# mLSTM gate arithmetic placed in the projection stage instead of attention, with eager evacuations, five raw buffers and shifted attention splits

## The chip, the cores and the metric

The kernel runs on 1 core of a Trainium2 chip. The metric is the device time of one execution in microseconds (us). Engines are named as in the profile: PE is the matmul engine (PEld its weight load), DVE the vector engine, ACT the scalar engine with its function tables, POOL the general engine, SP the engine whose queue issues nearly all DMAs here. PSUM is the memory that PE writes its products to.

## What is computed

One encoder layer on x of 2048 tokens by 1024 features, all in float32:

```python
h = rms_norm(x);  z = h @ W_in      # columns: mLSTM q|k|v|out-gate|16 gates, MLA latents, rotary key
qk  = silu(conv5(z_q|z_k))          # centred convolution over 5 tokens
y_a = sigmoid(o) * rms_norm(mlstm_fwd(q,k,v,i,f) + mlstm_bwd(...))   # 4 heads, chunks of 128 tokens
y_b = attention(4 heads, per-head RMSNorm on q and k, rotary part of 64)
x = x + concat(y_a, y_b) @ W_out
x = x + relu(rms_norm(x) @ W1)**2 @ W2
# mLSTM, per head and direction, before any product with q, k, v:
b = cumsum_in_chunk(log_sigmoid(f));  u = i - b;  cu = cummax(u)
m = running state over the 16 chunks (max/add);  M = max(cu, m)
w = exp(u - M_last);  it = exp(m - M);  gd = exp(-(b + M));  dec = exp(m - M_last)
```

The last three lines are the gate arithmetic, which this change moves. Its whole input is the 16 gate columns for 2048 tokens (c.G, 128 partitions); everything is 128 x 128 or smaller.

## The kernel before

Every float32 product is made of three PE matmuls of high and low parts (lines 68 to 70, `mm3`), so each operand is split: ACT casts the high part (L53), DVE or POOL subtracts the low part (L54). For the weights of the first stage, which also take a gain, L56 is ACT's cast and L57 DVE's low part.

Stages, in order of time:

- **Projection** (`phase_a`, 0 to 466 us). Two halves of 1024 tokens. A half begins with the 464 columns of gates and latents (`rest`: gate evacuation into c.G, L284 `zr`), and then come three blocks of eight products each: blk 0 is `z_v` (mLSTM values), blk 1 `z_qk` (transposed q and k, then the convolution), blk 2 `z_o` (output gate). Each product is 24 matmuls of 512 columns into one of two banks (`pz`, pool psZ), evacuated into `vo` or `zc`. Weights come as `raw` tiles (pool `a_raw`, 3 buffers), 8 to a block. Between them run the MLA steps (`tick`: latent norms, `cTh` splits, the k, v, q products into `pm`, transpositions of `kn`, `qn`, `qr`, `kr` into `pt`, stores of kT, qT, rT). `prep` transposes x into hh and hl. The order of instructions in this stage is not the order of the code: a tile scheduler sets it by priorities (code order, unless a block is marked with a priority offset), against its own model of the engines.
- **Attention** (`attention`, 467 to 1165 us). The order is written by hand: step g of 256, eight (s = 0 to 7) to each block of 256 queries, emits score, softmax, transposition and value products, and calls `next(work)` once on the mLSTM generator, which therefore fills the steps one yield at a time. That generator begins with `mlstm_prelude` (24 yields, the gate arithmetic), then `mlstm_steps`. The prelude's small matmuls and transpositions on PE go through `pm` banks, its arithmetic through DVE and ACT. `split_q` and `split_k` (ACT cast, POOL or DVE low parts) prepare the next queries and the next head.
- **Output projection and feed-forward** (from about 1160 us to the end): a hand-written order, where `weights()` splits W_out during attention's last steps, and `load_y(s)`, `load_x(s)` bring tile s of y and x into a ring of tiles.

All SP DMAs stand in one queue: a DMA that waits for its tile holds all behind it.

Of the kernel before, what the change touches and what calls it, by code (L numbers as in the profile page):

```python
# [8 lines left out]
F32 = mybir.dt.float32  # L9
# [57 lines left out]
def mm3(nc, out, ah, al, bh, bl, first, last):  # L67
    nc.tensor.matmul(out, ah, bh, start=first, stop=False)  # L68
    nc.tensor.matmul(out, ah, bl, start=False, stop=False)  # L69
    nc.tensor.matmul(out, al, bh, start=False, stop=last)  # L70
# [17 lines left out]
def scratch(c, ctx):  # L88
# [15 lines left out]
    c.d_dec = dr.tile([P, 1], F32, name="d_dec")  # L104
# [13 lines left out]
def phase_a(c):  # L118
    nc, tc = c.nc, c.tc
    with ExitStack() as st:  # L120
# [6 lines left out]
        rp = pool("a_raw", 3)  # L127
# [10 lines left out]

        def load_x(t):
            xt = kp.tile([P, D], F32, name=("wukh", "wukl")[t - 2]) if t in (2, 3) else xp.tile([P, D], F32, name="xt")  # L140
            for q, cs in ((nc.sync, slice(0, 512)), (nc.scalar, slice(512, D))) if t == 0 else ((nc.sync, slice(0, D)),):
                q.dma_start(xt[:, cs], c.x[t * P:(t + 1) * P, cs])
            return xt

        def prep(t, xt, hh, hl):

            if t >= NL:
                junk = ep.tile([P, D], BF16, name="xjunk", bufs=1)
# [6 lines left out]
            for g in range(2):  # L155
                pt = psT.tile([P, 4, P], F32, name="pt")
                for k in range(4):
                    nc.tensor.transpose(pt[:, k, :], xt[:, (4 * g + k) * P:(4 * g + k + 1) * P], c.ident)
                split(nc, hh[:, 4 * g:4 * g + 4, tt * P:(tt + 1) * P],
                      hl[:, 4 * g:4 * g + 4, tt * P:(tt + 1) * P], pt)  # L160
# [104 lines left out]
        def z_nat(hts, tl, w, n):  # L265
# [3 lines left out]
            for k in range(KD):  # L269
                mm3(nc, pz[:, :n], hh[:, k, ts], hl[:, k, ts], w[k][0][:, :n], w[k][1][:, :n],  # L270
                    k == 0, k == KD - 1)
            return pz

        def rest(t, hts, w):
            pz = z_nat(hts, t % 8, w, NR)
            for half, ci in ((0, t), (2, NT - 1 - t)):
                dst, zg, b = c.G[:, half:half + 2, :, ci], pz[:, half * 4:half * 4 + 8].rearrange(
                    "p (a h) -> p a h", a=2), bg[:, half * 4:half * 4 + 8].rearrange("p (a h) -> p a h", a=2)
                if t < NL:
                    nc.vector.scalar_tensor_tensor(dst, zg, rinv[:, t:t + 1], b, op0=ALU.mult, op1=ALU.add)  # L280
                else:
                    nc.vector.tensor_tensor(dst, zg, b, op=ALU.add)
            zr = zp.tile([P, 448], F32, name="zr")
            nc.scalar.activation(zr, pz[:, 16:NR], AF.Copy, scale=rinv[:, t:t + 1] if t < NL else 1.0)  # L284
# [16 lines left out]
        def mla_a1(t, zr):  # L301
# [17 lines left out]
            split(nc, ch, cl, pt[:, 0:3, :])  # L319
# [93 lines left out]
        def z_qk(j, ch, hts, w):  # L413
# [13 lines left out]
            if j == 0:  # L427
                nc.vector.tensor_tensor(zc[:, 4:516], pz, rbs[0], op=ALU.mult)
            else:
                nc.scalar.copy(zc[:, 4:516], pz)  # L430
# [39 lines left out]
        def z_v(t, hts, w):  # L470
            pz = z_nat(hts, t % 8, w, 512)
            o = ep.tile([P, 512], F32, name="vo")
            if t < NL:
                nc.vector.tensor_scalar(o, pz, rinv[:, t:t + 1], None, op0=ALU.mult)
            else:
                nc.vector.tensor_copy(o, pz)
            nc.sync.dma_start(c.d_v[t * P:(t + 1) * P, :], o)

        def z_o(t, hts, w):
            pz = z_nat(hts, t % 8, w, 512)  # L480
            o = ep.tile([P, 512], F32, name="vo")
            nc.scalar.activation(o, pz, AF.Sigmoid, scale=rinv[:, t:t + 1] if t < NL else 1.0)
# [37 lines left out]
        for half in range(2):  # L520
# [34 lines left out]
            for blk in range(3):  # L555
# [3 lines left out]
                for i in range(8):  # L559
# [35 lines left out]
def mlstm_prelude(c, psM):  # L595


    nc, tc = c.nc, c.tc
    H = P // 2
    with ExitStack() as st:  # L600
        pool = st.enter_context(tc.tile_pool(name="g_sb", bufs=1, reuse_waits="tile"))

        def bank():
            return psM.tile([P, 512], F32, name="pm")

        def sb(name, shape=(P, P)):
            return pool.tile(list(shape), F32, name=name)

        pg = bank()[:, 0:256].rearrange("p (a t) -> p a t", a=2)
        for j in range(2):  # L610
            nc.tensor.matmul(pg[0:H, j, :], c.G[:, j], c.ident, start=True, stop=True)
            nc.tensor.matmul(pg[H:P, j, :], c.G[:, 2 + j], c.rev, start=True, stop=True)
        yield
        f, li, e, w, ln, d = sb("f"), sb("li"), sb("e"), sb("w"), sb("ln"), sb("d")
        nc.vector.tensor_copy(f, pg[:, 1, :])
        nc.vector.tensor_copy(li, pg[:, 0, :])
        yield
        nc.scalar.activation(e, f, AF.Abs)
        nc.scalar.activation(e, e, AF.Exp, scale=-1.0)
        yield  # L620
        nc.vector.tensor_scalar(w, e, 1.0, None, op0=ALU.add)
        yield
        wi = sb("wi")
        nc.scalar.activation(ln, w, AF.Ln)
        nc.vector.tensor_scalar(d, w, 1.0, None, op0=ALU.subtract)
        nc.vector.tensor_tensor(d, e, d, op=ALU.subtract)
        nc.vector.reciprocal(wi, w)
        nc.vector.tensor_tensor(d, d, wi, op=ALU.mult)
        yield
        yield  # L630
        nc.vector.tensor_tensor(ln, ln, d, op=ALU.add)
        nc.vector.scalar_tensor_tensor(f, f, 0.0, ln, op0=ALU.min, op1=ALU.subtract)
        b, u, cu, gs = sb("b"), sb("u"), sb("cu"), sb("gs", (P, 2))
        nc.vector.tensor_tensor_scan(b, f, f, 0.0, op0=ALU.add, op1=ALU.bypass)
        yield
        nc.vector.tensor_tensor(u, li, b, op=ALU.subtract)
        nc.vector.tensor_tensor_scan(cu, u, u, -3.0e38, op0=ALU.max, op1=ALU.bypass)
        nc.vector.tensor_copy(gs[:, 0:1], b[:, P - 1:P])
        nc.vector.tensor_copy(gs[:, 1:2], cu[:, P - 1:P])
        yield  # L640
        yield
        yield
        pr = bank()[0:1, 0:256].rearrange("p (a t) -> p a t", a=2)
        for j in range(2):
            nc.tensor.transpose(pr[:, j, :], gs[:, j:j + 1], c.ident)
        yield
        g1, mr = sb("g1", (1, 2, P)), sb("mr", (1, 8, NT))
        nc.vector.tensor_copy(g1, pr)
        nc.vector.memset(mr, 0.0)
        for r in range(8):  # L650
            s = slice(r * NT, (r + 1) * NT - 1)
            nc.vector.tensor_tensor_scan(mr[:, r, 1:], g1[:, 1, s], g1[:, 0, s], 0.0, op0=ALU.max, op1=ALU.add)
        yield
        yield
        pm = bank()[:, 0:1]
        nc.tensor.transpose(pm, mr.rearrange("p r c -> p (r c)"), c.ident[0:1, 0:1])
        yield
        mp = sb("mp", (P, 1))
        nc.vector.tensor_copy(mp, pm)
        M, it, dec, gd, nl = c.gM, c.git, c.gdec, sb("gd"), sb("nl", (P, 1))  # L660
        nc.vector.tensor_scalar(M, cu, mp, None, op0=ALU.max)
        nc.vector.tensor_scalar(nl, M[:, P - 1:P], -1.0, None, op0=ALU.mult)
        nc.vector.tensor_tensor(gd, b, M, op=ALU.add)
        yield
        nc.scalar.activation(dec, mp, AF.Exp, bias=nl)
        nc.scalar.activation(w, u, AF.Exp, bias=nl)
        nc.scalar.activation(it, M, AF.Exp, scale=-1.0, bias=mp)
        nc.scalar.activation(gd, gd, AF.Exp, scale=-1.0)
        nc.sync.dma_start(c.d_dec, dec)
        yield  # L670
        x1, x2 = sb("x1", (P, 3, P)), sb("x2", (P, 2, P))
        p2 = bank()[:, 0:256].rearrange("p (a t) -> p a t", a=2)
        for j, t in enumerate((M, it)):
            nc.tensor.transpose(p2[:, j, :], t, c.ident)
        yield
        nc.vector.tensor_copy(x2, p2)
        p1 = bank()[:, 0:384].rearrange("p (a t) -> p a t", a=3)
        for j, t in enumerate((u, w, gd)):
            nc.tensor.transpose(p1[:, j, :], t, c.ident)
        yield  # L680
        nc.vector.tensor_copy(x1, p1)
        for par in range(2):
            nc.sync.dma_start(
                c.dec[par * 64:(par + 1) * 64],
                c.d_dec.rearrange("(a p c) o -> p o a c", p=2, c=NT)[par].to_broadcast((64, 4, NT)))
        yield
        p4 = bank()[0:H, 0:256].rearrange("p (a t) -> p a t", a=2)
        for j in range(2):
            nc.tensor.matmul(p4[:, j, :], x2[:, j, H:P], c.rev, start=True, stop=True)
        yield  # L690
        rv = c.grv
        nc.vector.tensor_copy(rv, p4)
        p3 = bank()[:, 0:192].rearrange("p (a t) -> p a t", a=3)
        nc.tensor.matmul(p3, c.rev, x1[:, :, H:P], start=True, stop=True)
        yield
        nc.vector.tensor_copy(c.gn[:, :, 0:H], x1[:, :, 0:H])
        nc.vector.tensor_copy(c.gn[:, :, H:P], p3)
        yield
        for d in range(2):
            for h in range(NH):  # L700
                r = slice(d * H + h * NT, d * H + (h + 1) * NT)
                rr = slice(h * NT, (h + 1) * NT)
# [1284 lines left out]
```

## Time and profile before

| | |
|---|---|
| median of 3 runs | 2597.55 us (2594.62 to 2598.93) |
| profiled execution, own time | 2595.53 us |
| its span | 2593.8 us |
| granted TensorE clock | 1.0 |
| PE busy | 2568.8 us (99%) |
| DVE, ACT, POOL busy | 1674.2, 1213.0, 396.0 us (65, 47, 15%) |

The span covers the first to the last instruction; the own time has 1.7 us more around it. Rows of the profile read: line of the kernel, engine, operation, output<-inputs, count, then busy time and mean ns, and the idle time just before with what ended it. In answers in order of time, a row begins with its start and its length in us. Buffer numbers are left out of names.

### The profile page before, as it was taken

The page shows a single profiled execution, that of the slowest core. Times are in us where ns is not written, and L with a number is a line of the kernel's source. Part 1 is how long each engine was busy: PE and PEld are TensorE (multiplying, and loading weights), DVE is VectorE, ACT ScalarE, POOL GpSimd, SP SyncE. Part 2 cuts the span into 40 slices and gives each one's busy share as a digit, 9 for nine tenths or more (in the row PEclk, how much of TensorE's full clock was granted, in tenths as well). Part 3 has the DMA queues.
Part 4 walks back from the last instruction along what each step waited for, and adds up shares of the span by engine and source line. Part 5 has one row for each costly group of instructions (what it writes and reads, how often), then busy time and mean ns, then how long its engine had stood idle before and what let it go on. Part 6 is the DMA issues. An engine that isn't in the chain of part 4 may idle for free. (4 is left out here: it accounts for less than half of the span.)

```text
span 2593.8 us, 37092 instructions
## 1 busy us (share of the span) xinstructions
PE 2568.8 (99%) x13232; PEld 2168.7 (84%) x13232; DVE 1674.2 (65%) x3206; ACT 1213.0 (47%) x2457; POOL 396.0 (15%) x438
## 2 busy tenths in 40 slices
PE   8999999999999999999999999999999999999999
PEld 7888887788888888898888888888888888888887
DVE  5585467666676667675458777877775477675443
ACT  6454444545656556572135554655554323332332
POOL 1111110123224214111000000000000133222000
PEclk9999999999999999999999999999999999999999
DMA  5334235366446555435674656754446644444542
GB/s 168 126 119 151 94 114 164 68 134 126 104 86 131 92 111 105 86 110 173 211 247 160 198 185 195 253 174 142 161 147 241 247 146 146 146 146 146 211 176 97
DMA packets 297757, 391.57 MB, mean 151 GB/s; under 512 B 32677, under 2 KB 186340, under 8 KB 297572
## 3 DMA queue, kind: packets, MB, share of 16 engines
q1 hardware_dynamic: 295108, 384.74, 50.2%
q10 hardware_dynamic: 2464, 4.46, 0.5%
q8 instruction: 104, 1.70, 0.3%
q14 instruction: 81, 0.66, 0.1%
HBM read 256.94 MB, written 132.17 MB: 150 GB/s over the span
## 5 line engine op out<-in xcount | busy, mean ns | idle before, releaser
L68 PE MATMUL pd<-w2h,uh 128*128 128x512 f32 x896 | 348.7, 389 | 0.1
L69 PE MATMUL pd<-w2l,uh 128*128 128x512 f32 x896 | 348.6, 389 | 0.0
L70 PE MATMUL pd<-w2h,ul 128*128 128x512 f32 x896 | 348.6, 389 | 0.0
L54 DVE TENSOR_TENSOR ul<-ur,uh 128x1024 fp32r<-128x1024 f32 x110 | 147.1, 1337 | 252.5 <-ACT uh L53 252.3
L53 ACT CAST uh<-ur 128x1024 fp32r<-128x1024 f32 x110 | 115.9, 1054 | 395.4 <-PE pd L69 381.3
L54 DVE TENSOR_TENSOR ptl<-ptp,pth 128x512 fp32r<-128x512 f32 x252 | 173.7, 690 | 183.0 <-ACT pth L53 176.1
L53 ACT CAST pth<-ptp 128x512 fp32r<-128x512 f32 x252 | 146.4, 582 | 241.7 <-PE ptp L1106 233.2
L1604 DVE TENSOR_TENSOR e<-pu,e 128x512 f32<-128x512 f32 x224 | 151.5, 689 | 98.3 <-PE pu L70 88.9
L1066 DVE TENSOR_SCALAR_CACHE_REDUCE p<-ps 128x512 f32<-128x512 f32 x256 | 174.9, 684 | 44.0 <-PE ps L1065 39.0
L68 PEld LDWEIGHTS pd<-w2h,uh 128*128 128x128 f32 x896 | 168.2, 188 | 35.5 <-DVE e L1604 0.5
L70 PEld LDWEIGHTS pd<-w2h,ul 128*128 128x128 f32 x896 | 168.2, 188 | 34.9
L69 PEld LDWEIGHTS pd<-w2l,uh 128*128 128x128 f32 x896 | 168.2, 188 | 34.9
L1764 POOL TENSOR_TENSOR r<-wr,r 128x512 f32<-128x512 f32 x48 | 85.8, 1788 | 620.8 <-DMA wr<-in_w 594.7
L1480 ACT CAST r<-w1raw 128x512 fp32r<-128x512 f32 x160 | 98.3, 615 | 121.9 <-PE pu L70 112.3
L68 PE MATMUL pz<-wh,hh 128*128 128x512 f32 (+1 forms) x384 | 150.2, 392 | 5.0 <-ACT hh L53 1.8
L1106 PE MATMUL ptp<-ident,p 128*128 128x128 f32 x1008 | 150.9, 273 | 1.3 <-ACT p L1077 0.9
L69 PE MATMUL pz<-wl,hh 128*128 128x512 f32 (+1 forms) x384 | 149.7, 390 | 1.7 <-DVE wl L57 1.6
L70 PE MATMUL pz<-wh,hl 128*128 128x512 f32 (+1 forms) x384 | 150.6, 392 | 0.0
L69 PE MATMUL pv<-ptl,vh 128*128 128x256 f32 x496 | 140.8, 284 | 2.4 <-DVE ptl L54 2.1
L68 PE MATMUL pv<-pth,vh 128*128 128x256 f32 x496 | 140.7, 284 | 0.0
L1607 ACT ACTIVATE e<-e 128x512 f32<-128x512 f32 x128 | 81.0, 633 | 127.1 <-DVE e L1604 120.6
L70 PE MATMUL pv<-pth,vl 128*128 128x256 f32 x496 | 140.3, 283 | 0.0
(441 smaller groups left out, 6587.0 us busy)
## 6 DMA issues: line engine op xcount, KB each, us to landing
d_u<-e SPq DMA_DIRECT2D x224, 256.0 KB
ur<-d_u SPq DMA_DIRECT2D x110, 512.0 KB
w1raw<-in_w SPq DMA_DIRECT2D x64, 512.0 KB
wr<-in_w SPq DMA_DIRECT2D x96, 256.0 KB
raw<-in_w_in SPq DMA_DIRECT2D x48, 256.0 KB
mb<-d_M SPq DMA_DIRECT2D x32, 256.0 KB
r<-in_x SPq DMA_DIRECT2D x16, 512.0 KB
d_x<-r SPq DMA_DIRECT2D x16, 512.0 KB
```

What stands on the lines that cost most here:

```text
L53: nc.scalar.copy(hi, src)
L54: (eng or nc.vector).tensor_tensor(lo, src, hi.bitcast(F32), op=ALU.subtract)
L68: nc.tensor.matmul(out, ah, bh, start=first, stop=False)
L69: nc.tensor.matmul(out, ah, bl, start=False, stop=False)
L70: nc.tensor.matmul(out, al, bh, start=False, stop=last)
L1066: nc.vector.tensor_scalar(probs[b, a][:, j, :], o, SCALE, None, op0=ALU.mult, op1=ALU.max, accum_out=maxes[b, a][:, j:j + 1])
L1106: nc.tensor.transpose(pt[:, k, :], p[:, j, k * P:(k + 1) * P], c.ident)
L1480: self.c.nc.scalar.copy(wh, src)
L1604: nc.vector.tensor_tensor(out, o, t, op=ALU.add)
L1607: nc.scalar.activation(t, t, AF.Relu)
L1764: nc.gpsimd.tensor_tensor(R, wr, R, op=ALU.subtract)
```

## The change

1. `mlstm_prelude` (24 yields in attention) is gone. `gate_arithmetic` does the same arithmetic in the second half of the projection, one step behind each of the eight value products. Its PE steps are put under `issue_after(c.last.ins)`, c.last being the last matmul of the newest z product, and its DVE and ACT work under a priority raised by 400. Its tiles take the slots of `zc`, `ot`, `acc`, `sg`, `kt` in the pool of the convolution (two buffers of zc and ot, one of the others), its PSUM banks come from psT (`pt`, two banks, shared with the transpositions). One transposition more brings `dec` into a row. Results go to DRAM (`d_gn`, 192 KB; `d_dec`; as before d_M and d_in), and attention starts with `load_gates`: three loads, then 4 yields in place of 24. The mLSTM generator therefore runs 20 steps earlier through all of attention.
2. Evacuations of PSUM in the projection stage are marked `urgent()` (priority raised by 400).
3. `a_raw` has 5 buffers instead of 3.
4. In attention, `split_q` is at s = 3 (5 before), `split_k` of parts 1, 2, 3 at s = 4, 6, 7 (4, 5, 6), and the next head's first value loads at s = 7 (6).
5. `load_y(2)` of the output projection is issued inside `weights()`, ahead of `load_x(0)`; before, after the end of attention.

```diff
@@ phase_a
-        rp = pool("a_raw", 3)
+        rp = pool("a_raw", 5)
+        def urgent():
+            return tc.high_priority(offset=400)
...
-                split(nc, hh[:, 4 * g:4 * g + 4, tt * P:(tt + 1) * P],
-                      hl[:, 4 * g:4 * g + 4, tt * P:(tt + 1) * P], pt)
+                with urgent():
+                    split(nc, hh[:, 4 * g:4 * g + 4, tt * P:(tt + 1) * P],
+                          hl[:, 4 * g:4 * g + 4, tt * P:(tt + 1) * P], pt)
...
-            split(nc, ch, cl, pt[:, 0:3, :])
+            with urgent():
+                split(nc, ch, cl, pt[:, 0:3, :])
...
+            with urgent():
+                if j == 0:
+                    nc.vector.tensor_tensor(zc[:, 4:516], pz, rbs[0], op=ALU.mult)
+                else:
+                    nc.scalar.copy(zc[:, 4:516], pz)
...
                     if blk == 0:
                         z_v(t0 + i, hts, w)
+                        if half == 1:
+                            if i == 0:
+                                gates = gate_arithmetic(c, ep, psT)
+                            next(gates, None)
@@ gate_arithmetic (new; the arithmetic as in mlstm_prelude)
+    (f, li, e, w), tf = four("zc")
+    (ln, d, wi, b), _ = four("zc")
+    (u, cu, M, it), _ = four("ot")
+    (gd, _, _, sm), tg = four("ot")
...
+    gn = tf[:, 0:3 * P].rearrange("p (a t) -> p a t", a=3)
+    def behind():
+        return c.tc.issue_after(c.last.ins)
+    with behind():
+        pg = bank()[:, 0:256].rearrange("p (a t) -> p a t", a=2)
...
+    with behind():
+        pm = bank()[:, 0:1]
+        nc.tensor.transpose(pm, mr.rearrange("p r c -> p (r c)"), c.ident[0:1, 0:1])
+    with c.tc.high_priority(offset=400):
+        nc.vector.tensor_copy(mp, pm)
+        nc.vector.tensor_scalar(M, cu, mp, None, op0=ALU.max)
+        nc.vector.tensor_scalar(nl, M[:, P - 1:P], -1.0, None, op0=ALU.mult)
+        nc.vector.tensor_tensor(gd, b, M, op=ALU.add)
+        nc.scalar.activation(dec, mp, AF.Exp, bias=nl)
+        nc.scalar.activation(w, u, AF.Exp, bias=nl)
+        nc.scalar.activation(it, M, AF.Exp, scale=-1.0, bias=mp)
+        nc.scalar.activation(gd, gd, AF.Exp, scale=-1.0)
+    yield
...
+    with behind():
+        p4 = bank()[0:H, 0:256].rearrange("p (a t) -> p a t", a=2)
...
+        nc.tensor.matmul(p3, c.rev, x1[:, :, H:P], start=True, stop=True)
+    with c.tc.high_priority(offset=400):
+        nc.vector.tensor_copy(rv, p4)
+        nc.vector.tensor_copy(gn[:, :, 0:H], x1[:, :, 0:H])
+        nc.vector.tensor_copy(gn[:, :, H:P], p3)
+    yield
+    nc.sync.dma_start(c.d_gn, gn)
...
@@ attention
-            yield from mlstm_prelude(c, psM)
+            load_gates(c)
+            for _ in range(4):
+                yield
...
-                    if s == 5:
+                    if s == 3:
                         split_q(hq, iq // 2)
...
-                    if i == 7 and s in (4, 5, 6):
-                        split_k(h + 1, s - 3)
-                        if s == 6:
+                    if i == 7 and s in (4, 6, 7):
+                        split_k(h + 1, {4: 1, 6: 2, 7: 3}[s])
+                        if s == 7:
@@ OutProj.weights
+            if k == 6:
+                self.load_y(2)
             if k > 5:
                 self.load_x(k - 6)
```

What the scheduler makes of it in the projection stage shows in the order of the built programs. First place: PE in blk 1 of the second half, where MLA's transpositions of the rotary parts (`qr`, `kr`) stand between two of the z_qk products (`pz`). Before, in one such place:

```order
L395 MATMUL pt<-ident,qn 128x128
L403 MATMUL pt<-ident,qr 128x128 x2
L403 MATMUL pt<-ident,kr 128x128 x2
L70 MATMUL pz<-hh,wl 128x512
L68 MATMUL pz<-hh,wh 128x512
L69 MATMUL pz<-hl,wh 128x512
```

In the changed kernel, PE, the start of the third z_qk product; L664 is the gates' transposition of the running state `mr`, which lies in the slot `kt`:

```order
L70 MATMUL pz<-hh,wl 128x512
L412 MATMUL pt<-ident,qr 128x128 x2
L412 MATMUL pt<-ident,kr 128x128 x2
L664 MATMUL pt<-ident,kt 128x1
L68 MATMUL pz<-hh,wh 128x512
L69 MATMUL pz<-hl,wh 128x512
```

Before, a product was under way on both sides of the small transpositions; now a product has ended ahead of them and the next one starts behind L664. What this product waits for is ACT's copy that frees its bank. On ACT, before, around copies of z_qk products in the second half (L430):

```order
L307 ACTIVATE mjunk,ms_3704<-zr 128x64
L430 COPY zc<-pz 128x512 x2
L441 ACTIVATE sg<-acc,vec 128x512
L430 COPY zc<-pz 128x512
L53 CAST cTh<-pt 128x384
```

And on ACT in the changed kernel, where L670 to L673 are the gates' four exponentials and L440 is the copy of z_qk's product into `zc`:

```order
L315 ACTIVATE mjunk,ms_3757<-zr 128x64
L672 ACT_TABLE_LOAD
L672 ACTIVATE ot<-ot 128x128
L670 ACTIVATE ot<-ot 128x1
L671 ACTIVATE zc<-ot 128x128
L673 ACTIVATE ot<-ot 128x128
L440 COPY zc<-pz 128x512
L53 CAST cTh<-pt 128x384
```

The exponentials, which need L664's result, now stand between the z_qk product and its copy. Second place: SP's queue and PE one product later. Before, SP at the end of an MLA step:

```order
L361 DMA d_va<-vn 128x512
L397 DMA d_qn<-qT 128x4x128
L407 DMA d_qr<-rT 64x2x128 x2
L407 DMA d_kr<-rT 64x2x128 x2
L448 DMA d_qkT<-ot 128x512
L391 DMA d_kn<-kT 128x4x128
```

In the changed kernel, SP at the MLA step during which the gates' last products are made:

```order
L370 DMA d_va<-vn 128x512
L400 DMA d_kn<-kT 128x4x128
L406 DMA d_qn<-qT 128x4x128
L416 DMA d_qr<-rT 64x2x128 x2
L416 DMA d_kr<-rT 64x2x128 x2
L700 DMA d_gn<-zc 128x384
L705 DMA d_M<-sg 16x128
```

And PE there, where L692 and L694 are the gates' last products, of which L694's result goes into the tile that L700 stores:

```order
L412 MATMUL pt<-ident,qr 128x128 x2
L412 MATMUL pt<-ident,kr 128x128 x2
L692 MATMUL pt<-rev,ot 64x128 x2
L694 MATMUL pt<-acc,rev 128x192
L68 MATMUL pz<-hh,wh 128x512
L69 MATMUL pz<-hl,wh 128x512
```

The store of d_gn is a new entry behind five stores of the MLA step, and its tile is a buffer of `zc`; the fourth z_qk product (`pz`, last rows) starts directly behind L694. Third place: SP at the end of attention, before:

```order
L1339 DMA r_13524<-in_x 128x1024
L1339 DMA r_13532<-in_x 128x1024
L1331 DMA r_13574<-d_ya 128x512
L1332 DMA r_13574<-d_yb 128x4x128
L1135 DMA d_yb<-y 128x256
```

and in the changed kernel:

```order
L1359 DMA r_13510<-d_ya 128x512
L1360 DMA r_13510<-d_yb 128x4x128
L1367 DMA r_13513<-in_x 128x1024
L1367 DMA r_13521<-in_x 128x1024
L1159 DMA d_yb<-y 128x256
```

The two loads of y now stand ahead of the two loads of x.

More of the change, by code (lines that the diff above doesn't have):

```diff
@@ L69, in mm3 @@
     nc.tensor.matmul(out, ah, bl, start=False, stop=False)
-    nc.tensor.matmul(out, al, bh, start=False, stop=last)
+    return nc.tensor.matmul(out, al, bh, start=False, stop=last)
 def consts(c, ctx):
@@ L103, in scratch @@
     c.d_in = dr.tile([2, NT, 2, 2, P], F32, name="d_in")
-    c.d_dec = dr.tile([P, 1], F32, name="d_dec")
+    c.d_dec = dr.tile([1, P], F32, name="d_dec")
+    c.d_gn = dr.tile([P, 3, P], F32, name="d_gn")
     c.d_C = dr.tile([NT - 1, P, 2, DV + 1], F32, name="d_C")
@@ L147, in prep @@
             if t >= NL:
-                junk = ep.tile([P, D], BF16, name="xjunk", bufs=1)
+                junk = ep.tile([P, D], BF16, name="kt", bufs=1)
                 ms = sp.tile([P, 1], F32, name="xms")
@@ L269, in z_nat @@
             for k in range(KD):
-                mm3(nc, pz[:, :n], hh[:, k, ts], hl[:, k, ts], w[k][0][:, :n], w[k][1][:, :n],
-                    k == 0, k == KD - 1)
+                c.last = mm3(nc, pz[:, :n], hh[:, k, ts], hl[:, k, ts], w[k][0][:, :n], w[k][1][:, :n],
+                             k == 0, k == KD - 1)
             return pz
@@ L278, in rest @@
                     "p (a h) -> p a h", a=2), bg[:, half * 4:half * 4 + 8].rearrange("p (a h) -> p a h", a=2)
[L279 to L282, printed above, removed]
+                with urgent():
+                    if t < NL:
+                        nc.vector.scalar_tensor_tensor(dst, zg, rinv[:, t:t + 1], b, op0=ALU.mult, op1=ALU.add)
+                    else:
+                        nc.vector.tensor_tensor(dst, zg, b, op=ALU.add)
             zr = zp.tile([P, 448], F32, name="zr")
-            nc.scalar.activation(zr, pz[:, 16:NR], AF.Copy, scale=rinv[:, t:t + 1] if t < NL else 1.0)
+            with urgent():
+                nc.scalar.activation(zr, pz[:, 16:NR], AF.Copy, scale=rinv[:, t:t + 1] if t < NL else 1.0)
             return zr
@@ L318, in mla_a1 @@
             cl = mp.tile([P, 3, P], F32R, name="cTl", bufs=2)
-            split(nc, ch, cl, pt[:, 0:3, :])
+            with urgent():
+                split(nc, ch, cl, pt[:, 0:3, :])
             mla_env[t] = [zr, ms3, ch, cl]
@@ L426, in z_qk @@
                 nc.vector.tensor_copy(zc[:, 0:4], carry[:, ch, :])
[L427 to L430, printed above, removed]
+            with urgent():
+                if j == 0:
+                    nc.vector.tensor_tensor(zc[:, 4:516], pz, rbs[0], op=ALU.mult)
+                else:
+                    nc.scalar.copy(zc[:, 4:516], pz)
             if last:
@@ L472, in z_v @@
             o = ep.tile([P, 512], F32, name="vo")
[L473 to L476, printed above, removed]
+            with urgent():
+                if t < NL:
+                    nc.vector.tensor_scalar(o, pz, rinv[:, t:t + 1], None, op0=ALU.mult)
+                else:
+                    nc.vector.tensor_copy(o, pz)
             nc.sync.dma_start(c.d_v[t * P:(t + 1) * P, :], o)
@@ L481, in z_o @@
             o = ep.tile([P, 512], F32, name="vo")
-            nc.scalar.activation(o, pz, AF.Sigmoid, scale=rinv[:, t:t + 1] if t < NL else 1.0)
+            with urgent():
+                nc.scalar.activation(o, pz, AF.Sigmoid, scale=rinv[:, t:t + 1] if t < NL else 1.0)
             nc.vector.tensor_tensor(o, o, gmo, op=ALU.mult)
@@ L592, in gate_tables @@
         c.nc.gpsimd.memset(t[:, :, DV:], 1.0)
[L595 to L702, printed above, removed]
-                nc.sync.dma_start(c.d_M[d, :, h], M[r, :] if d == 0 else rv[rr, 0, :])
-                nc.sync.dma_start(c.d_in[d, :, h % 2, h // 2], it[r, :] if d == 0 else rv[rr, 1, :])
-            yield
@@ L708, in mlstm_v, with load_gates @@
+def load_gates(c):
+    nc = c.nc
+    nc.sync.dma_start(c.gn, c.d_gn)
+    for par in range(2):
+        nc.sync.dma_start(
+            c.dec[par * 64:(par + 1) * 64],
+            c.d_dec.rearrange("o (a p c) -> p o a c", p=2, c=NT)[par].to_broadcast((64, 4, NT)))
 def mlstm_v(c, ch):
@@ L1876, in out_and_ffn @@
                 o.open(s_y.enter_context)
-                o.load_y(2)
                 last_store()
```

81 lines of the change are left out of this document (76 added, 5 removed).

## The prediction, made before the changed kernel was run

> **What bounds the kernel now.** I read the page first, then the waits of PE, then the windows of the projection stage, then single rows in order of time. Of the page:
>
> ```profile
> PE 2568.8 (99%) x13232; PEld 2168.7 (84%) x13232; DVE 1674.2 (65%) x3206; ACT 1213.0 (47%) x2457; POOL 396.0 (15%) x438
> PEclk9999999999999999999999999999999999999999
> ```
>
> PE is busy in all but 25 us of the 2593.8 of the span, at one clock. Moving PE's own gate steps from one PE-bound stage to another therefore changes nothing by itself; what counts is which of PE's idle moments go and which come. The waits of PE (what waited, for whom, us in total, times, longest):
>
> ```profile
> PE pt L198 <- DMA rows<-in_g_mix: 4.4, 1, 4.4
> PE pz L68 <- ACT hh L53: 1.8, 2, 1.3
> PE pz L68 <- ACT vo L482: 1.7, 1, 1.7
> PE pz L69 <- DVE wl L57: 1.6, 1, 1.6
> PE pm L68 <- ACT cTh L53: 1.3, 1, 1.3
> PE pm L674 <- ACT it L667: 1.1, 1, 1.1
> PE ypt L1348 <- DMA r<-d_ya: 1.1, 1, 1.1
> PE pz L68 <- ACT zr L284: 0.9, 1, 0.9
> PE pt L158 <- DVE hl L54: 0.8, 1, 0.8
> PE pz L68 <- ACT zc L430: 0.6, 1, 0.6
> PE pm L611 <- ACT vo L482: 0.5, 1, 0.5
> ```
>
> The whole prelude shows only in two rows, L674 and L611 (1.1 + 0.5): its other steps hide in attention. The windows of the projection stage (stretch, its length, then PE busy, PEld, DVE, ACT, POOL):
>
> ```profile
> 200.00:400.00 200.00, 198.91 (x1000) 170.15 (x999) 114.54 (x311) 90.00 (x271) 27.24 (x47) 1.00 0.37 116
> 400.00:470.00 70.00, 66.30 (x324) 54.37 (x323) 43.66 (x97) 32.60 (x87) 10.14 (x16) 1.00 0.58 172
> ```
>
> From 200 to 400 us PE lost 1.1 us, of which 0.9 is the zr wait: the blocks into which the gates go are nearly free of idle time now, so every new wait there is a loss, and little can be won there.
>
> **What it removes.** Edits 2, 3 and 5 and the prelude's leaving aim at single rows of that list. The urgent marks pull the copies forward on ACT and DVE: cTh 1.3, zr 0.9, zc 0.6 and the vo wait 1.7 I count as gone, since in the changed order each such copy stands earlier against the matmul that waits. Five raw buffers let most weight loads of the last block be issued before the queue fills with stores; the wl wait (1.6) goes. The two prelude rows go (1.1 + 0.5). load_y(2) goes ahead of load_x in SP's queue:
>
> ```profile
> 1164.30 7.34 SPq L1339 DMA_DIRECT2D r<-in_x  x2
> 1171.69 0.42 SPq L1331 DMA_DIRECT2D r<-d_ya  x1
> ```
>
> It was held 7.34 us by two loads that waited for their tiles; in front of them it starts up to 7 us earlier, and the 1.1 of ypt goes. What is late next is x's first tile, pushed back by one tile's release, to about 1171; DVE reads it only at 1176, so nothing follows on PE. Sum removed: 1.3 + 0.9 + 0.6 + 1.7 + 1.6 + 1.6 + 1.1 = 8.8 us. The hh and hl waits (1.3, 0.8, both at 36 us) stay, because the order of PE there is the same as before, and the 4.4 at the start is the first load. Lower bound of the removed sum: the three largest (vo, wl, cTh: 4.6) stay for other reasons, 4.2; upper bound 10.9, with hh and hl.
>
> **What it adds: the first gate wait (A).** Behind L664 on PE the third z_qk product follows at once, and it waits for ACT's copy of the first one into zc, which stands behind the four exponentials, which wait for what DVE makes of L664's result. Durations of the same instructions in the prelude and of the copies:
>
> ```profile
> L404 DVE COPY rT<-pt x16: 681/692/692, 93.1 to 436.0; 128x512 f32<-128x512 f32 x16
> 493.15 0.15 DVE L659 COPY mp<-pm 128x1 f32<-128x1 f32 x1
> 493.33 0.29 DVE L661 TENSOR_SCALAR M<-cu,mp 128x128 f32<-128x128 f32 x1
> 496.85 0.28 ACT L665 ACTIVATE dec<-mp,nl 128x1 f32<-128x1 f32 x1
> 497.82 0.56 ACT L53 CAST pth<-ptp 128x512 fp32r<-128x512 f32 x1
> L430 ACT COPY zc<-pz x12: 561/570/592, 160.5 to 431.3; 128x512 f32<-128x512 f32 x12
> ```
>
> PE's two pairs of rotary transpositions are ahead of L664, so DVE first copies rT (0.69), then mp (0.15) and M (0.29): about 1.1 with handovers. The four exponentials take 0.97 (496.85 to 497.82), the copy 0.57, and handing on to PE a little: 2.9 us, in which PE has nothing else. If rT's copy is done before, 2.1; if other ACT work falls between, 3.6.
>
> ACT also loads a function table right ahead of the exponentials. It can run while ACT waits for DVE, so I cost it at nothing here; if it can't, it adds its length. What a switch costs, in the prelude:
>
> ```profile
> 473.76 0.18 ACT L1077 ACTIVATION_READ_ACCUMULATOR p<-p,nm 128x1 f32 x1
> 473.96 1.28 ACT L624 ACT_TABLE_LOAD   x1
> 475.26 0.31 ACT L624 ACTIVATE ln<-w 128x128 f32<-128x128 f32 x1
> ```
>
> From the end of the work before to the first use 1.3 us pass, all of it the load. [...]
>
> **The second gate wait (B).** The fourth z_qk product stands directly behind L694 and waits for ACT's copy of the second one, whose zc buffer is the tile that d_gn's store reads. That store stands in SP's queue behind four stores of rT, which need DVE's rT copy, and the buffer is free only when the store has landed.
>
> ```profile
> 302.90 1.23 SPq L407 DMA_DIRECT2D d_qr<-rT  x2
> 304.17 1.26 SPq L407 DMA_DIRECT2D d_kr<-rT  x2
> L461 SPq DMA_DIRECT2D d_k<-kt x8: 360/404/608, 168.1 to 456.2; - x8
> 458.44 0.26 ACT L467 COPY kt<-pt 2x128 f32<-2x128 f32 x1 [2.14 <-DMA d_k<-kt]
> ```
>
> The four issues take 2.53 us (302.90 to 305.43). The nearest row for the landing is the store of kt, 192 KB like gn, issued at 456.2: ACT's next write to that tile came at 458.44, 2.2 us later. So behind the last rotary transposition: rT's copy 0.69, four issues 2.53, landing 2.2, zc copy 0.57, handovers 0.1: 6.1 us, less what PE itself does meanwhile in L692 and L694 with their own waits, 1.2: 4.9. Ends: 3.0 if the rT stores are issued well before, 6.7 if nothing of it overlaps and the landing takes half a us more. Queued behind the waiting copy on ACT are cTh's cast and the next kT, both read by PE later: they add to the small waits, next.
>
> **Smaller ones.** In the same stretch cTh, qT and rT copies on ACT and DVE now gate psT's two banks, which the gates share: 1.5 (0.5 to 2.5), the nearest rows being the 0.5 to 1.3 of single waits in the list. In the middle of the projection (about 230 to 260 us), in two places of the new order eight transpositions of x stand directly ahead of a product that reads their split; the same pattern costs 0.8 to 1.3 at 36 us; I take 1.05 each, 2.1 (0 to 3). One raw load now stands behind rT's stores, 0.5 (0 to 1.3, half of four issues). At the start of attention the copies of POOL stand where the prelude did, 0.4 (0 to 1). One more transposition, 0.1. The new loads of gn and dec: SP issues them just after 467 us, by the 2.2 us of the kt row they are there by 471, and PE's first mLSTM product is due some three steps later, 474: nothing, or up to 2 if the queue is late. The final drain and the steps of mLSTM are the same in number, 20 steps earlier.
>
> **Middle of attention (edit 4 and the 20 steps).** POOL's work at a head's boundary slows DVE:
>
> ```profile
> 981.25 3.89 DVE L876 SCALAR_TENSOR_TENSOR num<-num,rd,num 128x128 f32<-128x128 f32 x4
> 986.41 0.39 PE L69 MATMUL pv<-ptl,vh 128*128 128x256 f32 x1 [1.12 <-DVE ptl L54]
> ```
>
> There DVE needed nearly 1 us for each of these four small operations and PE then idled 1.12. POOL's splits are spread out now and other mLSTM steps meet the boundary: I take -1, with ends of -2 and +2.
>
> **The sum.** Added: 2.9 + 4.9 + 1.5 + 2.1 + 0.5 + 0.4 + 0.1 = 12.4. Removed: 8.8, and 1 in attention. Net +2.6 us: own time 2595.53 + 2.6 = 2598.1. The profiled execution was 2.0 below the median of the runs, 2597.55, so a median after of 2600.2.
>
> **Rivals.**
> - *The waits A and B are hidden* (the scheduler's order has more distance in time than I read, because stores are issued earlier and rT's copy is done). Then added is 2.1 + 0.5 + 0.1 and 0.3 of the small waits, 3.0, and removed 9.8: -6.8, or 2590.7. For it: 198.91 of 200 us busy shows how well that order did before. Against it: no matmul stands between L664 or L694 and the waiting product. It decides if A and B together stay under 2.5 us. Chance 0.15.
> - *The stop at B cools PE.* At the start, after 4.4 us of idle time, matmuls were issued at about half the rate for 8 us:
>
> ```profile
> 8.94 0.59 PE L69 MATMUL pz<-wl,hh 128*128 128x464 f32 x1
> 9.32 0.59 PE L70 MATMUL pz<-wh,hl 128*128 128x464 f32 x1
> ...
> 12.11 0.59 PE L69 MATMUL pz<-wl,hh 128*128 128x464 f32 x1
> ...
> 13.53 0.37 PE L69 MATMUL pz<-wl,hh 128*128 128x464 f32 x1
> 13.73 0.37 PE L70 MATMUL pz<-wh,hl 128*128 128x464 f32 x1
> ```
>
>   0.38 from start to start until past 12.1, against 0.20 from 13.5 on. If 4.9 us of idle time brings that back, the 8 us at half the rate cost 4 us more: 2604.2. No later stop of this trace was longer than 1.7, after which the rate was full, so it can't be excluded. [...] Chance 0.18.
> - *The waits come at their upper ends* (A 3.6, B 6.7, small ones 2.5, gn late by 2, the other 3.1 as above, only 6 removed and 1 in attention): +10.9, or 2608.5. Chance 0.1.
> - *The urgent marks and buffers do not do what they say*, with the removed sum at its lower bound of 4.2 and the added one as forecast: 12.4 - 4.2 - 1 = +7.2, or 2604.8. Its chance is counted in the 0.1 of the case above.
>
> **How the numbers follow.** Forecast 0.57, all within 0.2% (5.2 us), about what a measurement of this kernel can tell from no change; its own range is 2595 to 2602.7, by the ends of A, B and the attention term that nearly cancel, cut at that bound. The rivals share 0.15 below and 0.28 above. For eight in ten the range takes in half of the faster case and most of the slower ones: 2591.5 to 2607.
>
> **What would show it.** In the profile after: a wait of PE's pz for ACT zc (L440) of 2 to 3.6 us and one of 3 to 6.7 (put down to ACT, or to the store of d_gn on ACT), between 320 and 400 us; PE's idle time in that stretch up by 9; L674's row and the ypt row gone; vo, wl, cTh and zc rows gone or under 0.5. Wrong would be: the pz waits small, or the wl and vo rows still there, or slow matmul rows behind B; each moves the time as in its rival.

## The result and the profile after

The changed kernel takes 2612.44 us (median of 6 runs, 2611.14 to 2615.75) against 2596.22 us of the kernel before beside it: ratio 1.0064, interval 1.0053 to 1.0074, some 16 us slower. The profiled execution took 2611.14 us, with a span of 2609.4, 15.6 more than before. From its page:

```profile
span 2609.4 us, 37147 instructions
PE 2574.9 (99%) x13233; PEld 2172.0 (83%) x13233; DVE 1674.4 (64%) x3207; ACT 1214.8 (47%) x2459; POOL 411.6 (16%) x438
```

One matmul record more, yet PE is busy 6.1 us longer, and idle 34.5 us instead of 25.0. The two stretches with most of the loss, as windows (length, PE, PEld, DVE, ACT, POOL, then the granted clock, that is the share of the full TensorE clock that the trace records):

```profile
200.00:400.00 200.00, 187.86 (x932) 158.85 (x931) 107.21 (x322) 94.60 (x279) 29.02 (x51) 0.97 0.34 109
700.00:900.00 200.00, 197.09 (x1328) 176.54 (x1327) 131.12 (x341) 122.14 (x282) 56.37 (x59) 0.99 0.47 105
```

From 200 to 400 us PE idles 12.1 us instead of 1.1, and in both stretches the granted clock is under 1 (0.97 and 0.99). The waits of PE:

```profile
PE pz L68 <- ACT zc L440: 8.7, 2, 4.8
PE pv L69 <- DVE ptl L54: 4.6, 5, 2.9
PE pz L68 <- ACT hh L53: 3.2, 4, 1.2
PE pt L463 <- DVE ot L454: 1.0, 1, 1.0
PE pt L475 <- ACT kt L477: 0.8, 1, 0.8
```

Of the rows shown of before, those of vo, wl, the first cTh (0.2 is left), zr, `pm` L674 and `pm` L611 are gone, and zc has grown from 0.6 to 8.7. The second row was the second of before, too, which the prediction's list leaves out:

```profile
PE pv L69 <- DVE ptl L54: 2.1, 4, 1.1
```

The two waits that make up the 8.7, and the matmul rate behind the first of them, in order of time:

```profile
367.42 0.22 PE L664 MATMUL pt<-ident,kt 1*128 1x1 f32 x1
371.50 0.80 PE L68 MATMUL pz<-hh,wh 128*128 128x512 f32 x1 [3.86 <-ACT zc L440]
372.10 0.63 PE L69 MATMUL pz<-hl,wh 128*128 128x512 f32 x1
372.52 0.63 PE L70 MATMUL pz<-hh,wl 128*128 128x512 f32 x1
...
374.66 0.41 PE L69 MATMUL pz<-hl,wh 128*128 128x512 f32 x1
374.91 0.40 PE L70 MATMUL pz<-hh,wl 128*128 128x512 f32 x1
...
391.88 0.80 PE L68 MATMUL pz<-hh,wh 128*128 128x512 f32 x1 [4.82 <-ACT zc L440]
```

For some 3 us behind each stop a matmul starts every 0.43 us instead of 0.23: seven of them, 1.5 us lost each time. The third such place is in attention:

```profile
821.39 3.18 DVE L911 SCALAR_TENSOR_TENSOR sgt<-num,hrr,sgt 128x128 f32<-128x128 f32 x4 [2.99 <-POOL hrr L64]
825.84 0.58 PE L69 MATMUL pv<-ptl,vh 128*128 128x256 f32 x1 [2.91 <-DVE ptl L54]
```

POOL's `hrr` of the mLSTM stood behind the splits of q and k and a `kw`, DVE waited 2.99 us for it and then needed 3.18 us for four small operations; behind it, matmuls of 256 columns started every 0.21 us instead of 0.12 for 2.5 us, 1.4 lost. A fourth slow place has no long stop ahead of it. Around 236 us PE waited 0.71, 0.69 and 1.00 us within 3.8 us, at transpositions and splits of x, and then ran at half the clock for 3.41 us, in which matmuls of 464 columns started every 0.39 us instead of 0.21, 1.6 lost:

```profile
234.76:238.17 3.41, 1.35 (x6) 0.71 (x6) 3.41 (x7) 3.24 (x6) 0.00 (x0) 1.00 0.63 191
238.17:241.58 3.41, 3.38 (x11) 3.04 (x12) 2.50 (x4) 0.77 (x2) 0.00 (x0) 0.50 0.90 283
```

Sum: the three stops 3.86 + 4.82 + 2.91 = 11.6, and the four slow places 1.5 + 1.5 + 1.4 + 1.6 = 6.0, which is PE's longer busy time of 6.1. PE's other idle time, 34.5 - 11.6 = 22.9 us, is 2.1 shorter than the 25.0 of before; together that gives 15.5, against 15.6 of span.

### The profile page after: what moved, and what is told of

Its sections match the earlier page's. It is cut to its first block, busy times and chain, and to the rows that moved or that the text cites. A ratio compares the mean times of both kernels' runs of the same rounds, so it can differ in the third digit from the quotient of the medians.

```text
span 2609.4 us, 37147 instructions
## 1 busy us (share of the span) xinstructions
PE 2574.9 (99%) x13233; PEld 2172.0 (83%) x13233; DVE 1674.4 (64%) x3207; ACT 1214.8 (47%) x2459; POOL 411.6 (16%) x438
## 5 line engine op out<-in xcount | busy, mean ns | idle before, releaser
L54 DVE TENSOR_TENSOR ul<-ur,uh 128x1024 fp32r<-128x1024 f32 x110 | 137.2, 1248 | 247.0 <-ACT uh L53 246.7
L1792 POOL TENSOR_TENSOR r<-wr,r 128x512 f32<-128x512 f32 x48 | 99.4, 2070 | 606.7 <-DMA wr<-in_w 590.1
L1101 ACT ACTIVATE p<-p,nm 128x2048 f32<-128x2048 f32 x64 | 128.6, 2009 | 30.7 <-DVE nm L1094 30.7
```

What stands on the lines that cost most here:

```text
L54: (eng or nc.vector).tensor_tensor(lo, src, hi.bitcast(F32), op=ALU.subtract)
L1101: nc.scalar.activation(p, p, AF.Exp, bias=maxes.pop((b, a)), accum_out=dens[b][:, a:a + 1])
L1792: nc.gpsimd.tensor_tensor(R, wr, R, op=ALU.subtract)
```

## Experiments

Ratios are to the kernel before beside them, with a 95% interval. All traces quoted below are of the kernel named.

**The gate arithmetic alone undone** (`load_gates(c)` and 4 yields replaced by `yield from mlstm_prelude(c, psM)`, the stage's own arithmetic out).

> The kernel after, with edit 1 alone undone: the gate arithmetic is back in attention as mlstm_prelude (24 yields), edits 2 to 5 stay. Theory (the gates' two waits in the projection and the slow matmuls behind them make the loss): the waits of 3.86 and 4.82 us and two slow stretches of 1.5 go, the prelude's 1.6 comes back, so about 11 us less than 2612: 2601, and 2597 if the 2.9 us stop at 826 us with its slow stretch goes as well. Rival (the eager evacuations and raw buffers disturb the projection): still 2608 or more.

Ratio 1.0001 (0.9991 to 1.0010), as the theory has it when the stop at 826 us goes too. The whole loss belongs to edit 1; edits 2 to 5 together change nothing that can be measured. (The changed kernel also puts a scratch tile of x's norm, `xjunk`, into the slot `kt`; this run keeps that, so it costs nothing by itself.) Its windows have PE full where the changed kernel idled:

```profile
300.00:400.00 100.00, 100.00 (x489) 84.85 (x488) 62.84 (x180) 41.17 (x152) 17.00 (x25) 1.00 0.33 108
700.00:900.00 200.00, 200.00 (x1357) 179.33 (x1356) 132.82 (x344) 126.33 (x292) 67.83 (x69) 1.00 0.51 103
```

**The stored tile alone in a buffer of its own.**

```diff
-    gn = tf[:, 0:3 * P].rearrange("p (a t) -> p a t", a=3)
+    gn = ep.tile([P, 3, P], F32, name="gno", bufs=1)
-        rp = pool("a_raw", 5)
+        rp = pool("a_raw", 4)
```

> The kernel after, with the gates' result gn in a tile of its own instead of a zc buffer (and 4 raw buffers instead of 5, for the space). Theory: no zc copy waits for d_gn's store, so the 4.82 us wait and the 1.5 us of slow matmuls behind it go: 2612 - 6.3 = 2606. Rival (PE would wait there for something else anyway, since the product stands right behind the gates' last step): 2610 or more, with another releaser named.

Ratio 1.0091 (1.0075 to 1.0108): slower still. The scheduler made another order of it (with one raw buffer less), with three stops in place of two:

```profile
372.63 0.66 PE L324 MATMUL pt<-ident,cn 128*128 128x128 f32 x2 [4.64 <-DVE cn L320]
409.83 0.66 PE L324 MATMUL pt<-ident,cn 128*128 128x128 f32 x2 [4.82 <-DVE cn L320]
442.03 0.59 PE L68 MATMUL pz<-wh,hh 128*128 128x512 f32 x1 [4.22 <-ACT zc L440]
```

The rival won: taking the named wait away did not take the stop away. What the stops have in common is DVE or ACT late with the convolution's or the latents' work.

**Edit 4 undone, and the 20 steps undone.** First `split_q` and `split_k` at their old steps, then `for _ in range(24): yield` behind `load_gates`.

> The kernel after, with edit 4 alone undone: split_q at s = 5, split_k at s = 4, 5, 6 again. Theory (edit 4 puts POOL's splits of q and of the first k part ahead of the mLSTM norm hrr at the boundary at 820 us): the 2.9 us stop at 826 us and 1.5 of slow matmuls go: 2608. Rival (the 20 steps by which the mLSTM runs earlier bring hrr onto the splits): the stop stays, 2612 or a little more.

> The kernel after, with 24 yields behind load_gates instead of 4: the mLSTM runs in the same attention steps as before, with nothing in the first 24. Theory of the shift (the 20 steps make the stop at 826 us): the stop goes, 2608. Rival (edit 4 makes it): it stays, 2612.

Ratios 1.0063 (1.0048 to 1.0078) and 1.0060 (1.0045 to 1.0075): in time neither can be told from the changed kernel. The traces do tell. With the old split steps the stop is still there, 0.64 shorter; with 24 yields PE is all but full between 700 and 900 us, and its longest stop in all of attention behind the first 25 us is 0.34. The row of the one and the window of the other:

```profile
827.64 0.39 PE L69 MATMUL pv<-ptl,vh 128*128 128x256 f32 x1 [2.27 <-DVE ptl L54]
700.00:900.00 200.00, 199.82 (x1353) 178.82 (x1352) 133.58 (x343) 123.44 (x286) 61.28 (x63) 1.00 0.51 106
```

So the stop is made by the shift of the mLSTM against the splits, and not by edit 4, which at most lengthens it. The 4 us are there in the traces: from PE's wait for `rl` near 486 or 488 us to its wait at the first `ypt` near 1204 us pass 718.9 us in the changed kernel and 714.7 with 24 yields. They are not to be seen in the times: the trace of that run had 2.8 us more in the projection, up to attention the same program, 1.95 of it a stop at 48.5 us with half the clock behind it.

**The changed kernel again, and the zc tiles of the gates private.**

```diff
-    (f, li, e, w), tf = four("zc")
-    (ln, d, wi, b), _ = four("zc")
+    (f, li, e, w), tf = four("gf", 1)
+    (ln, d, wi, b), _ = four("gl", 1)
-        rp = pool("a_raw", 5)
+        rp = pool("a_raw", 3)
```

> The kernel after, unchanged, beside the others on one chip, since its ratio to before was taken elsewhere: 1.0064 by every theory, with the same two waits of 3.9 and 4.8 us.

> The kernel after, with the gates' two tiles that took the slots of zc in storage of their own (and 3 raw buffers, as before, for the space). ACT's copies of the z_qk products then stand ahead of the gates' exponentials in the built order, and no copy waits for d_gn's store. Theory (the shared zc buffers make both waits, and the waits the slow matmuls): both waits and both slow stretches go, 9.0 + 3.1: ratio to before 1.0064 - 0.0046 = 1.002. Rival (the gates' steps cost this wherever their tiles lie, by PSUM banks, ACT and DVE): 1.005 or more, with stops of like length elsewhere.

> As the kernel with the gates' own tiles, and 24 yields behind load_gates instead of 4, so that the mLSTM keeps its steps of before. Theory (both waits from the tiles, the stop at 826 us from the shift of 20 steps): the stop of 2.9 us with 1.5 of slow matmuls goes as well, ratio 1.002 - 0.0017 = 1.000. Rival (edit 4 makes that stop): no change against the kernel with 4 yields.

Ratios 1.0058 (1.0041 to 1.0074), 1.0046 (1.0031 to 1.0061) and, with 24 yields, 1.0041 (1.0026 to 1.0056); in time the last two can't be told apart, though the stop at 821 us (2.89) is gone from the trace of the last. With the zc tiles private the first wait is gone, the second has turned into a longer one for somebody else:

```profile
385.23 0.48 DVE L446 TENSOR_SCALAR acc<-zc,vec 128x512 f32<-128x512 f32 x1
...
386.57 0.35 DVE L382 SCALAR_TENSOR_TENSOR kn<-pm,r,gk 128x128 f32<-128x128 f32 x1
...
388.26 1.39 DVE L386 SCALAR_TENSOR_TENSOR qn<-pm,r,gq 128x192 f32<-128x192 f32 x4
389.57 0.74 DVE L448 SCALAR_TENSOR_TENSOR acc<-zc,vec,acc 128x512 f32<-128x512 f32 x1
390.23 0.35 DVE L320 TENSOR_SCALAR cn<-zr,r 128x256 f32<-128x256 f32 x1
...
390.72 0.66 PE L324 MATMUL pt<-ident,cn 128*128 128x128 f32 x2 [5.80 <-DVE cn L320]
```

The rows are DVE's, the last is PE's. The convolution of the first z_qk product (L446) begins at 385 us only, behind the gates' last products, which read x1 out of its tile `acc`; with it and the latents' norms ahead, `cn` is late and PE waits 5.80. So the theory of the zc buffers was too narrow, and the new one, argued here and put to the test next, is that all the tiles that the gates borrow from the convolution hold it back.

**All gate tiles private.**

```diff
-    (f, li, e, w), tf = four("zc")
...
+    gA = ep.tile([P, 4 * P], F32, name="gA", bufs=1)
+    gB = ep.tile([P, 4 * P], F32, name="gB", bufs=1)
+    sm = ep.tile([P, 8], F32, name="gsm", bufs=1)
+    f, li, e, w = (gA[:, k * P:(k + 1) * P] for k in range(4))
+    ln, d, wi, b = (gB[:, k * P:(k + 1) * P] for k in range(4))
+    u, cu, M, it = gA[:, 2 * P:3 * P], gA[:, P:2 * P], gA[:, 0:P], gA[:, P:2 * P]
...
+    gn = x1     # in gB; rv, x2 in gA; g1, mr, gd in gB
-        rp = pool("a_raw", 5)
+        rp = pool("a_raw", 3)
```

> The kernel after, with all the gates' tiles private: two tiles of 2 KB and a small one, laid out so that nothing of zc, ot, acc, sg or kt is used (3 raw buffers for the space); same arithmetic, same pins and priorities, same PSUM banks. Theory (it is the tiles shared with the convolution: with only zc freed, acc, sg and ot still held the convolution's DVE work back, which then stood in front of cn): the stops of 3.9, 4.8 or 5.8 us and their slow matmuls go, ratio to before 1.000 to 1.002, the rest being the stop at 826 us. Rival (the gates' steps on PE, in psT's two banks, make the stops wherever the tiles lie): a stop over 3 us between 360 and 400 us stays, ratio 1.004 or more.

> As e9_private, with 24 yields behind load_gates, so that the mLSTM keeps its steps of before. Theory: e9_private less the stop at 826 us and its slow matmuls, 4.4 us: ratio 0.0017 below it, 0.9985 to 1.0005. Rival (stops in attention are not set by the shift): equal to e9_private.

Ratios 1.0025 (1.0015 to 1.0035), where 1.002 at most was expected, and, with 24 yields, 0.9992 (0.9983 to 1.0002). The gates' steps go through the same two banks of PSUM, and the window is full, so the rival is out. The three raw buffers, which came with it, don't do this alone: the kernel with the zc tiles private has them too, and the stop of 5.80. With 4 yields the start of attention is not full (both rows of the kernel with 4 yields):

```profile
300.00:400.00 100.00, 100.00 (x493) 83.90 (x492) 65.09 (x200) 46.81 (x161) 16.80 (x25) 1.00 0.33 104
470.00:540.00 70.00, 63.23 (x411) 52.01 (x411) 41.65 (x110) 30.45 (x43) 10.30 (x14) 0.95 0.64 153
```

The first convolution of the second half begins at 366.15 us here, at 387.38 in the changed kernel, at 385.23 with only the zc tiles private (DVE's L446). What is left of the loss, 1.0025, is the stop at 816 us and a new wait:

```profile
476.64 0.43 SPq L725 DMA_DIRECT2D gn<-d_gn  x1
480.68 1.20 POOL L762 TENSOR_TENSOR kw<-knat,gn 128x256 f32<-128x256 f32 x2 [11.66 <-DMA gn<-d_gn]
481.35 1.13 PE L769 MATMUL pm<-v,kw 128*64 128x129 f32 x8 [6.77 <-POOL kw L762]
```

SP issues gn's load at 476.64, behind the projection's last store (472.55) and five loads of v and knat for the mLSTM, and PE's first mLSTM product is due 4 yields into attention: 6.77 us, with slow matmuls behind it (512 columns in 0.63 us against 0.39 ahead of it). With 24 yields it is not due before the load lands, and the stop at 816 us goes as well; the two kernels differ by 0.33%, 8.6 us, twice what was expected of the stop alone. A load of gn ahead of those of v and knat was not tried.

**Without the urgent mark on the split of x**, otherwise as the kernel with private tiles and 24 yields.

> As e10_private_24, without the urgent mark on the split of x (hh, hl) in the projection. Theory (that mark makes the stops at 48 us and 235 to 240 us, about 4 us in all, which the kernel before does not have): those stops go, ratio 0.0015 below e10_private_24. Rival (the stops come from the other urgent marks or the raw buffers): equal to it.

Ratio 0.9989 (0.9979 to 0.9999): equal to the one before it, and too near to 1 to call it faster than the kernel before. The mark was not the cause of the stops near 48 and 236 us: with it, the kernel with private tiles had none of them either, so this run had nothing to remove. All kernels with five raw buffers had both, none with three or four had any; that the fifth buffer makes them, by the order that the scheduler then finds, fits all of them, but no run changed it alone.

**The kernel before, for its trace on that chip.**

> The kernel before, for its trace on this chip, since the kernel with edits 2 to 5 alone showed 4.6 us less span than the first trace of before, but the same time as before on its own chip. By both theories the stops are those of the first trace; the span should be about 2590 to 2591, so that edits 2 to 5 are worth about 1 to 2 us and not 4.6.

Span 2592.8 us, a little above what was expected; the waits are those of the first trace but for cTh (1.94 instead of 1.30) and ypt (2.34 instead of 1.12). Beside the 2589.2 of the kernel with edits 2 to 5 alone it would leave them 3.6 us, while the timed runs say 0.3 us slower, give or take 2.6. The two traces are single executions: the one of edits 2 to 5 was the fastest of its ten (2590.99, median 2592.55), this one was slower than the median of before on its chip (2594.62, median 2593.48). What the edits are worth stays open within the interval of the timed runs.

**How long a stop slows PE.** Behind the end of the kernel before, bursts of matmuls with stops between them:

```diff
+    for n in STOPS:      # n = 2 to 30
+        pb = ps.tile([P, 512], F32, name="sp")
+        for k in range(60):
+            nc.tensor.matmul(pb, w, x, start=k == 0, stop=k == 59)
+        nc.vector.tensor_copy(u, pb[:, 0:P])
+        for _ in range(n):
+            nc.vector.tensor_scalar(u, u, 1.0, None, op0=ALU.mult)
+        w = sb.tile([P, P], F32R, name="sw2", bufs=2)
+        nc.vector.tensor_copy(w, u)
```

> The kernel before, with 14 bursts of 60 matmuls of 512 columns behind the whole program, and between them stops of growing length (a chain of small DVE operations that the next burst waits for), about 1 to 8 us. Theory (a stop of PE beyond some length near 2.9 us brings back about 3 us of issue at half the rate): bursts behind stops up to about 2 us start at full rate, those behind stops over 3 us start with about 7 slow matmuls, always the same number, and lose 1.5 us. Rival (the slow stretch grows with the stop, up to the 8 us at the program's start): more slow matmuls behind longer stops.

Four of the thirteen restarts, each as the row of its first matmuls, merged, in a window that ends 0.6 to 2 us behind the restart:

```profile
2640.48 0.94 PE L1965 MATMUL sp<-sx,sw 128*128 128x512 f32 x3 [2.83 <-DVE sw L1970]
2657.43 2.05 PE L1965 MATMUL sp<-sx,sw 128*128 128x512 f32 x4 [3.09 <-DVE sw L1970]
2696.14 2.38 PE L1965 MATMUL sp<-sx,sw 128*128 128x512 f32 x7 [3.61 <-DVE sw L1970]
2846.54 2.04 PE L1965 MATMUL sp<-sx,sw 128*128 128x512 f32 x4 [8.58 <-DVE sw L1970]
```

Three matmuls in 0.94 us behind 2.83 us of idle time, four in 2.05 behind 3.09. By the starts of all matmuls, the stops of 1.17, 2.31 and 2.83 us cost nothing beyond themselves, and each of the ten from 3.09 to 8.58 us brought 7 to 13 slow matmuls and lost 1.4 to 2.7 us, without growing with the stop. Behind the one of 3.61 the slow stretch came only after four matmuls at full rate. So the theory's limit near 2.9 us fits these bursts, its constant seven matmuls and 1.5 us do not, and neither does the rival. In the other traces the limit does not hold either: the last section has what they show.

## Why the prediction was wrong

The forecast was 2600.2 us, 2.6 more than before, with 0.57 for no change; measured were 16 us more, 15.6 in span. Of the 13.0 us between 2.6 and 15.6, 6.1 are PE's longer busy time, all but 0.1 of it matmuls at half the clock, the stop in the middle of attention is 2.9, and waits A and B together are 0.9 more than forecast. All other terms together shortened the time by 2.1 us instead of 5.2, which is the last 3.1. A and B themselves came nearly as forecast. The step that failed most is the one that left the slow matmuls out of the sum, as a rival with one place; next come the sign of the term for attention, the table load at nothing, and the small waits.

- *Wait A*, forecast 2.9 (2.1 to 3.6), was 3.86. The step that failed in it is the table load costed "at nothing", on the ground that it can run while ACT waits for DVE. ACT was not waiting: it was at the latents' squares (L315) until 368.59, just as long as DVE needed for M (L667, to 368.61), and the load came behind both.

```profile
368.32 0.29 DVE L667 TENSOR_SCALAR ot<-ot 128x128 f32<-128x128 f32 x1
368.40 0.19 ACT L315 ACTIVATION_READ_ACCUMULATOR mjunk<-zr 128x1 f32 x1
368.61 1.28 ACT L672 ACT_TABLE_LOAD   x1
369.90 0.40 ACT L672 ACTIVATE ot<-ot 128x128 f32<-128x128 f32 x1
```

  All 1.28 us lay on the path; without them the wait would have been 2.6. The ground itself holds: in the trace of before, the load at 476.10 us began 0.02 us behind the ACT work ahead of it, and its user came only 1.23 us behind its end. In the rows above ACT went on 0.01 us behind the load.
- *Wait B*, forecast 4.9, was 4.82, by the steps as written: d_gn was issued at 389.08 behind four rT stores, and ACT's copy into its tile began 2.2 us later.

```profile
386.44 1.24 SPq L416 DMA_DIRECT2D d_qr<-rT  x2
387.74 1.25 SPq L416 DMA_DIRECT2D d_kr<-rT  x2
389.08 0.54 SPq L700 DMA_DIRECT2D d_gn<-zc  x1
391.24 0.59 ACT L440 COPY zc<-pz 128x512 f32<-128x512 f32 x1 [3.27 <-DMA d_gn<-zc]
```

- *The slow matmuls*, a rival with 0.18 and one place, came in four places: 1.5 us behind A, 1.5 behind B, 1.4 at 826 us and 1.6 at 238 us, 6.0 in all, where the sum has nothing. The price was taken from the program's start (4 us a time) and the place from B alone, though the trace of before left open what any stop over 1.7 us does, so that A, at 2.9, should have been counted too. That waits of 1.00 us at most, close together, would be followed by the same, as at 238 us, no row of before showed.
- *The middle of attention*, forecast -1 with an end at +2, had the wrong sign: 2.91 plus the slow matmuls. The wait that grew there, `pv` for `ptl`, is the one that the prediction's list of waits left out. Its row showed DVE slow beside POOL at a head's boundary (four operations of L876 in 3.89 us, 3.74 of it with POOL busy, where the median of all 64 is 0.35 each), and the shift of 20 steps moved another mLSTM step, with `hrr`, onto a place behind the splits. Edit 4, from which the prediction hoped for relief there, brought none: without it the stop was 2.27 instead of 2.91 us.
- *Small waits*, forecast 1.5, were 0.24 and 0.42; instead the convolution, held back, ended late, and PE waited 1.74 us for `ot` and `kt` at 468 us, a wait that the prediction did not have and that is gone with all gate tiles private. Seen from there, its reading of A and B was of the last link only: it named the zc buffer and not the convolution's other tiles, which the kernels with gn or zc alone freed show to be as binding.
- *Removed*, forecast 8.8: those rows are gone, but for 0.2 of cTh. New ones of the same kind came (hh 1.24 at 48 us, 2.4 at 236 us where 2.1 was forecast, ypt 0.61), and edits 2 to 5 together brought nothing in time.
- *gn's load* cost nothing in the changed kernel, as forecast, but that was luck. It was to be issued just after 467 us and read at 474; it was issued at 485.05, and PE's first mLSTM product ran at 490.68, with score products to fill the time until then. Where the rest of the projection was faster, the same load cost 6.77 us.

## What to carry over

Work that is moved to a stage with idle engines also borrows that stage's buffers, and a borrowed buffer is held from its first write to the landing of its last store (d_gn's, issued at 389.08 us, let ACT go on at 391.24): count what is queued for it, on every engine. Idle time of PE close together cost more than itself here: some 2 us of it within 3.4 us, in one stop or in three, was followed by half the clock and 1.4 to 2.7 us more. Small waits that lay apart, under 1.5 us of idle time in such a stretch, were followed by full clock. Where a scheduler sets the order, freeing the one buffer that a trace names may only hand the wait on; the test is to free all that the moved work shares.

## What was not expected of the hardware

In these traces the length of a stop alone does not tell whether the matmuls behind it are slow. A stop of 2.83 us cost nothing more in the sweep, and 2.89 with all tiles private nothing either, while 2.91 and 2.88 in two runs of the changed kernel brought the full slow stretch, 2.27 with the old split steps brought one 1.0 us behind the restart, and at 238 us three waits of 1.00 us at most did it. The clock that the traces record has an order in it. In the changed kernel the stretches at half the clock are 3.41 us long, the third 6.83, apart from the one at the program's end, and begin on one grid: at 238.17, 371.29, 388.36 and 825.26 us, which lie 39, 5 and 128 times 3.413 us apart.

What goes with it in these traces is how long PE idles within one stretch of that grid. With the old split steps the whole stop of 2.27 us lies in one stretch, PE is busy for 1.14 of 3.41 us, and the next is at half the clock:

```profile
825.19:828.60 3.41, 1.14 (x10) 0.96 (x9) 3.38 (x8) 0.18 (x1) 3.41 (x3) 1.00 0.27 93
828.61:832.02 3.41, 3.41 (x19) 3.41 (x18) 2.19 (x6) 2.47 (x3) 1.33 (x3) 0.50 0.83 199
```

With all tiles private and 4 yields the longer stop falls across a border of the grid, 1.68 us on one side and 1.21 on the other, and the clock stays full:

```profile
815.62 0.39 PE L69 MATMUL pv<-ptl,vh 128*128 128x256 f32 x1 [2.89 <-DVE ptl L54]
810.99:814.40 3.41, 1.73 (x11) 1.24 (x8) 3.25 (x5) 1.59 (x4) 2.69 (x3) 1.00 0.22 67
814.41:817.82 3.41, 2.21 (x19) 2.21 (x20) 3.38 (x10) 1.43 (x1) 0.00 (x0) 1.00 0.42 116
817.82:821.23 3.41, 3.41 (x26) 3.10 (x25) 1.46 (x4) 3.05 (x7) 2.15 (x2) 1.00 1.03 289
```

Over all fourteen traces, without the first and last 12 us of each, the 34 stretches at full clock in which PE idled 1.93 us or more were all followed by one at half the clock, and of the more than 10,000 with less than 1.50 none was; between the two, 10 were and 15 were not. In the changed kernel the four that were had 3.41, 2.33, 2.06 and 1.52 us, and the next, 1.43 from 466.86 us on, was not; in the kernel before the longest, 1.59 from 33.33 us on, was not. The ends of matmuls are modelled, so the limit is no sharper than that, and no run was built to test it. One and the same program had a slow stretch in one run and not in the next: the kernel before had none between its start and its end in its first trace and one in its second, at 1175.93 us, with its wait for ypt 2.34 us instead of 1.12. The grid lay elsewhere too: counted back in steps of 3.413 us from the half clock at the end of the first trace, 2593.33 us, its nearest border was near 1176.9. Such a stretch, 1.4 us or more at the places measured above, no edit made, and it limits how small a difference a single trace can show.
